# Hybrid block kernel on one core: where g_ffn, the decay weights and two k, q products stand at its start

## The chip, the cores and the metric

The kernel runs on one core of a Trainium2 chip. Its time is in device microseconds (us), the median of several runs. One more execution was taken by the hardware profiler; its time is given beside the median, and all rows below are of that execution. The engines are named TensorE (PE in the rows, PEld for its weight loads), VectorE (DVE), ScalarE (ACT), GpSimd (POOL) and SyncE (SP, which here only issues loads and stores).

## The reference

One layer of a backbone block over 512 latent tokens with a prefix of 256 context tokens, 1024 wide, in float32:

```python
mod_lat = jnp.split(jax.nn.silu(c) @ w_ada[l] + b_ada[l], 6, axis=-1)
mod_ctx = jnp.split(jax.nn.silu(c_ctx)[None, :] @ w_ada[l] + b_ada[l], 6, axis=-1)
pl = project(modulate(rmsnorm(x, g_mix[l]), sh1, sc1), w_in[l], w_dec_up[l], b_dec[l])
pc = project(modulate(rmsnorm(ctx, g_mix[l]), sh1c, sc1c), w_in[l], w_dec_up[l], b_dec[l])
...
zd = jnp.einsum('btdr,drk->dbtk', dd, w_dec_up) + b_dec[:, None, None, :]
log_a = jax.nn.log_sigmoid(zd.astype(jnp.float32)) / DECAY_TAU
...
x = x + gt1[:, None, :] * mix_l
x = x + gt2[:, None, :] * swiglu(modulate(rmsnorm(x, g_ffn[l]), sh2, sc2), w_ffn_in[l], w_ffn_out[l])
return rmsnorm(x, g_final)
```

`project` multiplies the modulated tokens by `w_in`, whose columns are q, k, v, g, the low-rank decay dd (2 x 16 columns), three parts of a short convolution and two branch gates. q, k, v and the decay feed a gated linear attention of 4 heads, scanned in both directions from the context's final states. Its output, gated, and the convolution's are projected, summed and added to x; then comes a SwiGLU sub-layer.

## The kernel before

**Products.** A float32 product is made of three: each operand is split into a rounded high part (`h_...`, a ScalarE copy) and a low part (`l_...`, a VectorE subtraction), and TensorE adds high x high, high x low and low x high (`mm3`). So weights that have landed (`r_...`) pass ScalarE and VectorE before TensorE can take them.

**Order.** From `pinned[0] = True` (L469) up to the end of the attention, the instructions of TensorE, ScalarE and VectorE run in the order of the code; each engine takes its own strictly in turn. Ahead of that line and for the loads, a scheduler sets the order. SP issues the loads. Each has one of eight semaphores in turn, and waits until the earlier load of the same semaphore has landed.

**The start.** Small vectors are loaded as rows of 128 numbers into `vrow` (`small_vectors`, L176): g_mix in rows 0 to 7, g_ffn in 8 to 15, b_ada in 16 to 63, then g_head, b_dec and w_conv up to row 97. A first transpose `vps` (L471) turns rows 0 to 63 into columns of `vec`:

```python
vps = bank("vps")
tr(vps[:, :64], vrow[:64, :P], ident[:64, :64])
dve.tensor_copy(vec[:, :64], vps[:, :64])
normed(0, xts[0])
```

A second one, `vps2` in `head0_gather`, turns the rest. Behind `vps` come the latent tokens: `normed` scales a tile of 128 tokens by its root mean square, `turn` transposes it (`xtp`, TensorE) into `xsT`. Then `ada_rows(0)` multiplies c and c_ctx by the first half of w_ada's shift and scale columns (`ada`, eight tiles `wa` of 512 KB), `mod_cols` turns the row (`adar`) into columns (`adac`, `modT`, `gs`), `warm` does nine products of zeros, and `modulate(f)` makes `h`, tile f of the modulated tokens transposed (eight tiles of 128 channels). `w0_split` splits the weights of head 0 (`r_w`, four sets `wrs` of 256 channels, of which three buffers exist).

**Head 0's gather** (L502) goes through the eight tiles: `gather_v` adds tile k to v and the decay dd of the four latent token tiles, `gather_kq` to k and q. At k = 3 the second half of w_ada (`ada_rows(1)`, 16 loads) comes in, and tiles 4 to 7 are modulated. The context follows in `head0_gather`; there `wdu_split` splits the decay weights `wraw` (w_dec_up, eight loads of 16 rows) into `wdu`.

**Behind it**, `ddt` turns dd into `ddT`, and `decays` multiplies it by `wdu` (the product `z`) and scans the decays. Meanwhile TensorE does `g_tile(0, j)`, in single steps that `fill(n, hd)` puts between the stages. `SPLITS0` names the steps of that fill ahead of which a unit of the next weights is split (`split_unit`; here the two halves of head 1's v weights, `h_v` and `l_v`). The rest (four heads, convolution, projections, SwiGLU) is not touched.

Of the kernel before, what the change touches and what calls it, by code (L numbers as in the profile page):

```python
# [42 lines left out]
R_GM, R_GF, R_BA, R_GH, R_BD, R_WC, R_N = 0, 8, 16, 64, 66, 74, 98  # L43
# [3 lines left out]
def hybrid_block(ctx: ExitStack, tc: tile.TileContext, x, c, ctxt, c_ctx, w_ada, b_ada, g_mix, w_in,  # L47
                 w_dec_up, b_dec, g_head, w_gla_out, w_conv, w_conv_out, w_mix_out, g_ffn,
                 w_ffn_in, w_ffn_out, g_final, out):
    nc = tc.nc  # L50
# [14 lines left out]
    def u2(name, dt=F32, shape=(P, 512)):  # L65
        return up.tile(list(shape), dt, tag="u2", name=name, bufs=NU)
# [17 lines left out]
    def bank(name, shape=(P, 512)):  # L84
        return ps.tile(list(shape), F32, tag="ps", name=name, bufs=3)

    def gbank(name, shape=(P, 512)):
        return ps.tile(list(shape), F32, tag="pg", name=name, bufs=5)
# [17 lines left out]
    def f32(ap):  # L106
        return ap.bitcast(F32)
# [39 lines left out]
    def mm(*a, **k):  # L147
        pe_pin(nc.tensor.matmul(*a, **k))  # L148

    def tr(*a):  # L150
        pe_pin(nc.tensor.transpose(*a))

    def mm3(o, a, b, start, stop):
        mm(o, a[0], b[0], start=start, stop=False)
        mm(o, a[0], b[1], start=False, stop=False)
        mm(o, a[1], b[0], start=False, stop=stop)
# [19 lines left out]
    def small_vectors(vs):  # L176
        for r0, src in vs:
            n = src.shape[1] // P
            for d in range(src.shape[0]):
                nc.sync.dma_start(vrow[r0 + d * n:r0 + (d + 1) * n, :P], src[d:d + 1, :].rearrange("o (r f) -> (o r) f", f=P))  # L180

    small_vectors(((R_GM, g_mix), (R_BA, b_ada)))

    eps = cst.tile([P, 1], F32, name="eps")
    nc.vector.memset(eps, EPS)
# [47 lines left out]
    def token_load(i):  # L233
        if i < NT:
            xt = hp.tile([P, D], F32, tag="xt", name=f"xt{i}", bufs=4)
            nc.sync.dma_start(xt, x[i * P:(i + 1) * P, :])
        else:
            xt = wp.tile([P, D], F32, tag="raw", name=f"xt{i}", bufs=4)
            nc.sync.dma_start(xt, ctxt[(i - NT) * P:(i - NT + 1) * P, :])
        return xt  # L240
# [7 lines left out]
    def turn(i, xt, dst, j):  # L248
        for hh_ in range(2):
            tp = gbank(f"xtp{i}_{hh_}", (P, 4, P))  # L250
            for k in range(4):
                tr(tp[:, k, :], xt[:, (hh_ * 4 + k) * P:(hh_ * 4 + k + 1) * P], ident)
            (act_.copy if hh_ == 0 else dve.tensor_copy)(dst[hh_][:, :, j * P:(j + 1) * P], tp)
# [4 lines left out]
    def ada_load(hf):  # L258

        us = []  # L260
        for k in range(KT):
            src = w_ada[k * P:(k + 1) * P, :2 * D].rearrange("p (s f) -> p s f", s=2)[:, :, hf * 512:(hf + 1) * 512]
            if hf == 1:
                ts = [(uo if s_ else uh)(f"wa{k}{s_}") for s_ in range(2)]
                for s_ in range(2):
                    nc.sync.dma_start(ts[s_], src[:, s_, :])
            else:
                if k % 2 == 0:
                    t = wp.tile([P, 2, 512], F32, tag="raw", name=f"wa0{k}", bufs=4)
                else:  # L270
                    t = hp.tile([P, 2, 512], F32, tag="wa", name=f"wa0{k}", bufs=4)
                nc.sync.dma_start(t, src)
                ts = [t[:, s_, :] for s_ in range(2)]
            us.append(ts)
        return us

    def ada_rows(hf, us):

        rows = gbank(f"ada{hf}")
        for k in range(KT):  # L280
            for s_ in range(2):
                g_ = 64 * (k % 2) + 32 * s_
                mm(rows[g_:g_ + 32, :], cw[:, k, :], us[k][s_], start=k < 2, stop=k >= KT - 2)
        rsb = u2(f"adar{hf}")
        dve.tensor_copy(rsb, rows)
        return rsb
# [5 lines left out]
    def mod_split(src, f, j, hi, lo):  # L292
        g_, sh = gs[:, f, j:j + 1], modT[:, f, 0, j:j + 1]
        act_.activation(hi, src, AF.Identity, scale=g_, bias=sh)
        dve.tensor_scalar(src, src, g_, sh, ALU.mult, ALU.add)
        dve.tensor_sub(lo, src, f32(hi))

    def mod_cols(hf, rsb):
        cp = gbank(f"adac{hf}")
        for i in range(4):  # L300
            mm(cp[:, 4 * i:4 * i + 4], rsb[:, i * P:(i + 1) * P], sel.rearrange("p s c -> p (s c)"), start=True, stop=True)
        fs = slice(4 * hf, 4 * hf + 4)
        ba = vec[:, R_BA:R_BA + 2 * KT].rearrange("p (s f) -> p f s", s=2)
        dve.tensor_tensor(modT[:, fs], cp[:, 0:16].rearrange("p (f s c) -> p f s c", f=4, s=2),
                          ba[:, fs, :].unsqueeze(3).broadcast_to([P, 4, 2, 2]), ALU.add)

        dve.scalar_tensor_tensor(gs[:, fs, :], modT[:, fs, 1, :], 1.0,
                                 vec[:, R_GM + 4 * hf:R_GM + 4 * hf + 4].unsqueeze(2).broadcast_to([P, 4, 2]), ALU.add, ALU.mult)

    def modulate(f):  # L310
        mod_split(xsT[:, f, :], f, 0, *h[f])

    def wdu_load():
        wraw = u2("wraw")
        whi_ = u2("wdhi", F32R)
        for d in range(2):
            for r in range(4):
                nc.sync.dma_start(wraw[d * 64 + r * 16:d * 64 + r * 16 + 16, :], w_dec_up[0, d])
        return wraw, whi_

    def wdu_split(wraw, whi_):
        dve.tensor_copy(whi_, wraw)
        for d in range(2):
            a = d * 64
            dve.tensor_copy(wdu[a:a + 32, :], f32(whi_)[a:a + 32, :])
            dve.tensor_sub(wdu[a + 32:a + 64, :], wraw[a + 32:a + 64, :], f32(whi_)[a + 32:a + 64, :])
# [107 lines left out]
    def w0_load(p_):  # L434

        r = hp.tile([P, 2, NW + 256], F32, tag="wr", name=f"r_w0{p_}", bufs=3)
        for d0, c0, n in ((0, CV, HV), (HV, CD, 32), (NW, CK, P), (NW + P, CQ, P)):
            nc.sync.dma_start(r[:, :, d0:d0 + n], w_in[p_ * 256:(p_ + 1) * 256, c0:c0 + n].rearrange("(a p) b -> p a b", p=P))
        return r

    def w0_at(k, a, e):
        return tuple(w_[:, k % 2, a:e] for w_ in w0[k // 2])

    def gather_v(os, src, k):
        for i, o in enumerate(os):
            mm3(o[:, :NW], tuple(w_[:, i * P:(i + 1) * P] for w_ in src[k]), w0_at(k, 0, NW), k == 0, k == KT - 1)
# [10 lines left out]

    vo = [bank(f"v0_{NC_}")]

    xts = [token_load(i) for i in range(NT)]  # L460
    was = [ada_load(0)]
    wrs = [w0_load(p_) for p_ in range(2)]
    was.append(ada_load(1))
    wrs += [w0_load(p_) for p_ in range(2, 4)]
    small_vectors(((R_GF, g_ffn), (R_GH, g_head), (R_BD, b_dec[0]), (R_WC, w_conv[0])))
    xcs = [token_load(NT + i) for i in range(NC_)]
    wdu_ = wdu_load()
    lat = (xsT[:, :4, :], xsT[:, 4:, :])
    pinned[0] = True  # L469
    vps = bank("vps")  # L470
# [3 lines left out]
    for i in range(NT):  # L474
        if i + 1 < NT:
            normed(i + 1, xts[i + 1])
        turn(i, xts[i], lat, i)
    rsb = ada_rows(0, was[0])
    mod_cols(0, rsb)
    warm(9)  # L480
# [17 lines left out]
    def gather_kq(k):  # L498
        gather(ko, NW, h, k)
        gather(qo, NW + P, h, k)  # L500

    for k in range(KT):  # L502
        if k == 3:
            rsb = ada_rows(1, was[1])
        gather_v(vo, h, k)
        if k == 3:
            mod_cols(1, rsb)
            modulate(4)
            w0_split(2)
            modulate(5)  # L510
            modulate(6)
            w0_split(3)
            modulate(7)
            for i in range(NC_):
                normed(NT + i, xcs[i])
        gather_kq(k)
        if k == 5:
            xcT = [wp.tile([P, 4, TC], F32, tag="raw", name=f"xcT{i}", bufs=4) for i in range(2)]
            for i in range(NC_):
                turn(NT + i, xcs[i], xcT, i)  # L520
            for f in range(KT):
                mod_ctx(f)
# [12 lines left out]
    def head0_gather():  # L535
        for k in range(KT + 2):
            if k < KT:
                gather_v(vc, hc, k)
            if k >= 2:
                gather(kc, NW, hc, k - 2, TC)  # L540
            if k == 5:
                ddt(NC_, NC_ + NT)
                wdu_split(*wdu_)
                vps2 = gbank("vps2")
                tr(vps2[:, :R_N], vrow[:R_N, :P], ident[:R_N, :R_N])
                dve.tensor_copy(vec[:, 64:], vps2[:, 64:R_N])
# [275 lines left out]
    split_unit()  # L822
    head0_ctx()

    SPLITS0 = (3, 7)
    SPLITS = (3, 34, 60, 61)
    SPLITS1 = (25, 34, 60, 61)
    SPLITS3 = (8, 15, 24, 29, 42, 46, 48, 58, 71, 76, 79, 96)
# [2 lines left out]
    def fill(n, hd):  # L831
        nonlocal nwork
        for _ in range(n):
            if nwork in (SPLITS0 if hd < 0 else SPLITS1 if hd == 0 else SPLITS if hd + 1 < H else SPLITS3):
                split_unit()
# [297 lines left out]
    for ch in range(2):  # L1133
# [9 lines left out]
        for t in range(NT):  # L1143
# [8 lines left out]
            else:  # L1152
# [4 lines left out]
                r = rstd_of(ss, 1, D, f"fin{t}")  # L1157
# [32 lines left out]
```

## Time and profile before

| | |
|---|---|
| median of 3 runs (1046.06 to 1047.03) | 1046.06 us |
| the profiled execution's own time | 1044.44 us |
| its span, first to last instruction | 1042.7 us |
| TensorE busy | 985.5 us, 95% of the span |
| VectorE, ScalarE busy | 543.4 us (52%), 382.1 us (37%) |
| GpSimd busy | 2.2 us |
| mean granted TensorE clock | 0.996 |

Busy shares are means over the whole span; a stretch in which an engine stands still is found in the waits and the timeline. In rows, "L102" and "L148" are helpers that record every VectorE and ScalarE operation, or every product, of the pinned part, so the tile's name tells them apart. A row "out<-in" names the tile written and those read. The granted clock is 1.00 at TensorE's higher level (2.4 GHz) and 0.50 at its lower (1.2 GHz).

### The profile page before, as it was taken

What the parts mean: (1) busy time and instruction counts of PE and PEld (TensorE: products, weight loads), DVE (VectorE), ACT (ScalarE), POOL (GpSimd) and SP (SyncE); (2) the same over time, 40 slices, a digit from 0 to 9 for tenths busy, and PEclk for the clock granted to TensorE, in tenths of its full rate; (3) what the DMA queues carried; (4) which work ended last, traced back from release to release, by engine and by line L of the source; (5) the groups of instructions that cost most, each with busy time, mean ns of one, the idle gap of its engine ahead of it and who ended that gap; (6) DMA issues with size and microseconds to landing.
All of it is one profiled execution on the core that took longest, in us unless ns stands there. A gap on an engine that the chain in (4) does not pass through costs nothing.

```text
span 1042.7 us, 12813 instructions
## 1 busy us (share of the span) xinstructions
PE 985.5 (95%) x5204; PEld 823.9 (79%) x5204; DVE 543.4 (52%) x838; ACT 382.1 (37%) x602; POOL 2.2 (0%) x10
## 2 busy tenths in 40 slices
PE   0488999999999999999999999999999999999997
PEld 0267888888788888888888888898888888888886
DVE  1257687677655677778734444743334233332423
ACT  2145656455835422232322232453233232321323
POOL 0000000000000000000000000000000000000000
PEclk9999999999999999999999999999999999999999
DMA  9504111211234667666723222232323323232302
GB/s 322 197 23 112 51 45 58 62 34 49 61 101 132 202 181 223 183 184 200 230 82 105 96 87 99 78 102 83 120 81 101 101 82 118 84 121 81 109 33 81
DMA packets 105536, 117.16 MB, mean 112 GB/s; under 512 B 5395, under 2 KB 89477, under 8 KB 105477
## 3 DMA queue, kind: packets, MB, share of 16 engines
q1 hardware_dynamic: 105476, 116.34, 36.5%
q8 instruction: 41, 0.67, 0.3%
q14 instruction: 19, 0.15, 0.0%
HBM read 114.22 MB, written 2.10 MB: 112 GB/s over the span
## 4 chain that ended last, share of the span: by engine, by line
PE 91%; DMA 3%; ACT 2%; DVE 2%; issue 1%; SPq 0%; ACTq 0%; DVEq 0%
PE f L148 23%; PE fo L148 10%; PE v L148 6%; PE yc L148 4%; PE yg L148 4%; PE gb L148 4%; PE cb L148 4%; PE ch L148 4%; PE cc L148 4%; PE ga L148 4%; PE g L148 4%; PE mx L148 3%; PE kl L148 2%; PE q L148 2%; PE o L148 2%; PE F L148 2%
## 5 line engine op out<-in xcount | busy, mean ns | idle before, releaser
L148 PE MATMUL f<-h,h_fa 128*128 128x512 f32 (+1 forms) x384 | 111.0, 372 | 0.2 <-DVE h L102 0.2
L148 PE MATMUL f<-h,h_fb 128*128 128x512 f32 (+1 forms) x384 | 110.2, 372 | 0.0
L148 PEld LDWEIGHTS f<-h,h_fa 128*128 128x128 f32 x384 | 70.2, 188 | 13.2 <-DVE h L102 0.8
L148 PEld LDWEIGHTS f<-h,h_fb 128*128 128x128 f32 x384 | 70.0, 188 | 12.4
L148 PE MATMUL f<-h,l_fb 128*128 128x512 f32 (+1 forms) x192 | 71.3, 371 | 0.0
L148 PE MATMUL f<-h,l_fa 128*128 128x512 f32 (+1 forms) x192 | 71.3, 371 | 0.0
L102 DVE TENSOR_TENSOR l_fa<-r_fa,h_fa 128x1024 fp32r<-128x1024 f32 x22 | 26.9, 1225 | 74.6 <-ACT h_fa L102 74.6
L102 DVE TENSOR_TENSOR l_fo<-r_fo,h_fo 128x1024 fp32r<-128x1024 f32 x22 | 26.9, 1225 | 68.7 <-ACT h_fo L102 68.7
L148 PE MATMUL fo<-h_fo,ah 128*128 128x512 f32 x154 | 60.5, 393 | 0.0
L148 PE MATMUL fo<-l_fo,ah 128*128 128x512 f32 x154 | 60.5, 393 | 0.0
L148 PE MATMUL fo<-h_fo,al 128*128 128x512 f32 x154 | 60.4, 392 | 0.0
L907 DVE SCALAR_TENSOR_TENSOR acc<-r_wa,c,acc 128x256 f32<-128x256 f32 x112 | 54.1, 483 | 9.9 <-DMA r_wa<-in_w_ada_dram 7.1
L102 ACT CAST h_fo<-r_fo 128x1024 fp32r<-128x1024 f32 x22 | 23.1, 1051 | 71.0 <-PE fo L148 27.4
L148 PEld LDWEIGHTS f<-h,l_fb 128*128 128x128 f32 x192 | 36.2, 188 | 6.3
L148 PEld LDWEIGHTS f<-h,l_fa 128*128 128x128 f32 x192 | 36.1, 188 | 6.3
L148 PE MATMUL g<-h,h_g 128*128 128x512 f32 x128 | 40.9, 401 | 0.0
L148 PE MATMUL gb<-h,h_gb 128*128 128x512 f32 x128 | 40.0, 394 | 0.0
L148 PE MATMUL cb<-h,h_cb 128*128 128x512 f32 x128 | 39.7, 391 | 0.0
L148 PE MATMUL cc<-h,h_cc 128*128 128x512 f32 x128 | 39.6, 390 | 0.0
L148 PE MATMUL ch<-h,h_ch 128*128 128x512 f32 x128 | 39.5, 390 | 0.0
L148 PE MATMUL ga<-h,h_ga 128*128 128x512 f32 x128 | 39.5, 390 | 0.0
L148 PE MATMUL v<-h_v,h 128*128 128x256 f32 x192 | 36.3, 285 | 0.0
(296 smaller groups left out, 2249.2 us busy)
## 6 DMA issues: line engine op xcount, KB each, us to landing
r_wa<-in_w_ada_dram SPq DMA_DIRECT2D x32, 512.0 KB, 4.8
r_fa<-in_w_ffn_in_dram SPq DMA_DIRECT2D x22, 512.0 KB, 3.6
r_fb<-in_w_ffn_in_dram SPq DMA_DIRECT2D x22, 512.0 KB
r_fo<-in_w_ffn_out_dram SPq DMA_DIRECT2D x22, 512.0 KB, 3.6
wa<-in_w_ada_dram SPq DMA_DIRECT2D x8, 512.0 KB, 9.4
wa<-in_w_ada_dram SPq DMA_DIRECT2D x16, 256.0 KB, 4.8
r_g<-in_w_in_dram SPq DMA_DIRECT2D x8, 512.0 KB
r_gb<-in_w_in_dram SPq DMA_DIRECT2D x8, 512.0 KB, 3.8
```

The lines of the kernel that those rows point to most:

```text
L102: return lambda *a, **k: pin(getattr(self.engine, op)(*a, **k))
L148: pe_pin(nc.tensor.matmul(*a, **k))
L907: nc.vector.scalar_tensor_tensor(acc, w_[:, k, :], ck, acc, ALU.mult, ALU.add)
```

## The change

g_ffn is loaded with g_mix and b_ada at the front. The eight loads of w_dec_up are issued by GpSimd instead of SP, called ahead of the tokens' loads, and `wdu_split` stands ahead of the first w_ada product instead of in `head0_gather`. In the gather, k and q of the third tile (k = 2) are done behind v of the fourth. `SPLITS0` moves the two splits by two steps of the fill.

```diff
-    small_vectors(((R_GM, g_mix), (R_BA, b_ada)))
+    small_vectors(((R_GM, g_mix), (R_GF, g_ffn), (R_BA, b_ada)))
...
-                nc.sync.dma_start(wraw[d * 64 + r * 16:d * 64 + r * 16 + 16, :], w_dec_up[0, d])
+                nc.gpsimd.dma_start(wraw[d * 64 + r * 16:d * 64 + r * 16 + 16, :], w_dec_up[0, d])
...
+    wdu_ = wdu_load()
     xts = [token_load(i) for i in range(NT)]
...
-    small_vectors(((R_GF, g_ffn), (R_GH, g_head), (R_BD, b_dec[0]), (R_WC, w_conv[0])))
+    small_vectors(((R_GH, g_head), (R_BD, b_dec[0]), (R_WC, w_conv[0])))
     xcs = [token_load(NT + i) for i in range(NC_)]
-    wdu_ = wdu_load()
...
         turn(i, xts[i], lat, i)
+    wdu_split(*wdu_)
     rsb = ada_rows(0, was[0])
...
         gather_v(vo, h, k)
+        if k == 2:
+            continue
         if k == 3:
             mod_cols(1, rsb)
+            gather_kq(2)
             modulate(4)
...
                 ddt(NC_, NC_ + NT)
-                wdu_split(*wdu_)
...
-    SPLITS0 = (3, 7)
+    SPLITS0 = (5, 9)
```

In SP's queue before, behind the 16 loads of w_ada's second half, stood the third set of head 0's weights, then g_ffn, the other vectors, the decay weights, the context's tokens (`xt`) and the fourth set:

```order
L438 DMA r_w_205<-in_w_in_dram 128x2x256
L438 DMA r_w_205<-in_w_in_dram 128x2x32
L438 DMA r_w_205<-in_w_in_dram 128x2x128 x2
L180 DMA vrow<-in_g_ffn_dram 8x128
L180 DMA vrow<-in_g_head_dram 2x128
L180 DMA vrow<-in_b_dec_dram 4x128 x2
L180 DMA vrow<-in_w_conv_dram 8x128 x3
L318 DMA wraw<-in_w_dec_up_dram 16x512 x8
L239 DMA xt_222<-in_ctx_dram 128x1024
L239 DMA xt_224<-in_ctx_dram 128x1024
L438 DMA r_w_210<-in_w_in_dram 128x2x256
```

Now g_ffn is the fourth load of the program, ahead of b_ada and of the first tokens; the fourth weight set stands right behind the third, and the decay weights are gone from this queue:

```order
L167 DMA c_rows<-in_c_dram 8x128
L168 DMA c_rows<-in_c_ctx_dram 8x128
L180 DMA vrow<-in_g_mix_dram 8x128
L180 DMA vrow<-in_g_ffn_dram 8x128
L180 DMA vrow<-in_b_ada_dram 48x128
L236 DMA xt_150<-in_x_dram 128x1024
```

The front of that queue was the same before but for the g_ffn row. On VectorE, at head 0's decay, the split of the decay weights (`wdhi`, `wdu`) stood ahead of `vec`, g's and head 0's splits, and a v split ahead of the context's ddT:

```order
L102 TENSOR_TENSOR wdu<-wraw,wdhi 32x512
L102 COPY vec<-vps_743 128x34
L102 TENSOR_TENSOR l_g_0_771<-r_g_0_676,h_g_0_770 128x1024
L102 TENSOR_TENSOR l_g_1_778<-r_g_1_678,h_g_1_777 128x1024
L102 TENSOR_TENSOR vl_0_785<-v_0_645,v_0_784 128x256
L102 TENSOR_TENSOR st_136<-v_0_645,ddh_788 128x4x16
L102 TENSOR_TENSOR vl_0_785<-v_1_646,v_0_784 128x256
L102 TENSOR_TENSOR st_136<-v_1_646,ddh_794 128x4x16
L102 TENSOR_TENSOR l_v_0_807<-r_v_0_680,h_v_0_806 128x1024
L102 CAST ddT<-ddt_815 128x256
L102 TENSOR_SCALAR la_820<-z_821,vec 128x256
```

In the changed kernel `vec` follows right behind the latent ddT, and the v split has gone behind the four operations on z (`la`):

```order
L102 CAST ddT<-ddt_737 128x512
L102 COPY vec<-vps_743 128x34
L102 TENSOR_TENSOR l_g_0_771<-r_g_0_681,h_g_0_770 128x1024
L102 TENSOR_TENSOR l_g_1_778<-r_g_1_683,h_g_1_777 128x1024
L102 TENSOR_TENSOR vl_0_785<-v_0_650,v_0_784 128x256
L102 TENSOR_TENSOR st_137<-v_0_650,ddh_788 128x4x16
L102 TENSOR_TENSOR vl_0_785<-v_1_651,v_0_784 128x256
L102 TENSOR_TENSOR st_137<-v_1_651,ddh_794 128x4x16
L102 CAST ddT<-ddt_809 128x256
L102 TENSOR_SCALAR la_814<-z_815,vec 128x256
```

The five operations on the decay weights now stand, on the same engine, between the last copy of the transposed tokens and the copy of the first w_ada row:

```order
L102 COPY xsT<-xtp_1_309 128x4x128
L102 CAST wdhi<-wraw 128x512
L102 CAST wdu<-wdhi 32x512
L102 TENSOR_TENSOR wdu<-wraw,wdhi 32x512
L102 CAST wdu<-wdhi 32x512
L102 TENSOR_TENSOR wdu<-wraw,wdhi 32x512
L102 COPY adar_337<-ada_320 128x512
L102 TENSOR_TENSOR modT<-adac_339,vec 128x16
```

There the copy of the row, and all that follows it, waits behind them for the loads of GpSimd's queue.

## Rows read from the trace of the kernel before

**Rows 1.** The page: busy us (share of the span), instructions.

```profile
PE 985.5 (95%) x5204; PEld 823.9 (79%) x5204; DVE 543.4 (52%) x838; ACT 382.1 (37%) x602; POOL 2.2 (0%) x10
```

**Rows 2.** Waits to 170 us: who, for whom: us, times, longest.

```profile
PE vps L151 <- DMA r_w<-in_w_in_dram: 34.1, 1, 34.1
```

**Rows 3.** Timeline, 0 to 75 us: start, us, instruction [idle before, releaser].

```profile
3.83 0.54 POOL L201 TENSOR_SCALAR_AFFINE_SELECT m<-m 128x128 f32<-128x128 f32 x2
...
7.24 0.29 ACT L102 ACTIVATE rs_x<-ss,eps 128x1 f32<-128x1 f32 x1
...
33.29 0.30 SPq L180 DMA_DIRECT2D vrow<-in_g_ffn_dram  x1
...
37.16 0.34 PE L151 MATMUL vps<-ident,vrow 64*128 64x64 f32 x1 [34.12 <-DMA r_w<-in_w_in_dram]
...
38.67 3.44 PE L151 MATMUL xtp<-ident,xt 128*128 128x128 f32 x16 [1.18 <-DVE xt L102]
...
45.76 3.64 PE L148 MATMUL ada<-wa,cw 128*32 128x512 f32 x32
45.86 0.69 DVE L102 COPY xsT<-xtp 128x512 f32<-128x512 f32 x1 [0.65 <-PE xtp L151]
```

**Rows 4.** Waits of SP's queue up to 130 us.

```profile
SPq L438 <- DMA wa<-in_w_ada_dram: 7.5, 12, 1.0
```

**Rows 5.** Timeline of SP's queue, 20 to 21.5 us.

```profile
20.71 0.37 SPq L438 DMA_DIRECT2D r_w<-in_w_in_dram  x1
```

**Rows 6.** A window: PE, PEld, DVE, ACT, POOL busy, clock, DMA, GB/s.

```profile
10.00:20.00 10.00, 0.00 (x0) 0.00 (x0) 0.00 (x0) 0.00 (x0) 0.00 (x0) 1.00 1.05 388
```

**Rows 7.** The chain that ended last, 40 to 120 us: start, us, what.

```profile
45.83 3.62 PE ada L148 x32
...
55.21 1.72 PE v L148 x11
...
62.89 0.70 PE kl L148 x3
...
69.66 0.80 PE adac L148 x8
...
72.95 1.30 DVE l_w L102
```

**Rows 8.** Timeline, 95 to 107 us: head 0's decay.

```profile
96.02 0.42 DVE L102 CAST wdhi<-wraw 128x512 fp32r<-128x512 f32 x1
...
98.75 0.19 DVE L102 COPY vec<-vps 128x34 f32<-128x34 f32 x1
...
103.52 0.30 PE L151 MATMUL ddt<-ident,st 128*128 128x128 f32 x1 [0.92 <-ACT st L102]
...
104.64 1.23 DVE L102 TENSOR_TENSOR l_v<-r_v,h_v 128x1024 fp32r<-128x1024 f32 x1 [1.27 <-ACT h_v L102]
105.78 0.42 DVE L102 CAST ddT<-ddt 128x256 fp32r<-128x256 f32 x1
...
106.25 0.76 PE L148 MATMUL z<-ddT,wdu 64*128 64x256 f32 x4 [2.43 <-DVE ddT L102]
```

**Rows 9.** Windows ahead of and behind z.

```profile
101.80:106.20 4.40, 0.94 (x4) 0.28 (x2) 2.44 (x5) 2.25 (x7) 0.00 (x0) 1.00 0.82 228
107.00:110.40 3.40, 3.40 (x11) 2.71 (x10) 3.05 (x5) 3.38 (x6) 0.00 (x0) 0.56 0.60 152
```

**Rows 10.** Loads up to 110 us: count, KB each, us to landing.

```profile
wa<-in_w_ada_dram SPq DMA_DIRECT2D x8, 512.0 KB, 9.4
...
wraw<-in_w_dec_up_dram SPq DMA_DIRECT2D x8, 32.0 KB, 1.7
```

**Rows 11.** VectorE's groups to 75 us: count, busy us, mean ns.

```profile
L102 DVE TENSOR_SCALAR xt<-xt,rs_x 128x1024 f32<-128x1024 f32 x4 | 3.0, 753 | 0.1
L102 DVE COPY xsT<-xtp 128x512 f32<-128x512 f32 x4 | 2.8, 688 | 1.9 <-PE xtp L151 1.9
```

## The prediction

> **What bounds the kernel now.** I first read the page's busy times: TensorE works 95% of the span [rows 1], so only a stretch in which it stands still can give back time, and I looked for those. The waits, longest first, have one that stands out: the small transpose `vps` stood 34.1 us [rows 2]. The timeline shows why. TensorE did its first transpose at about 3 us, and `vps` (L471, the first pinned instruction) started at 37.16 [rows 3]; everything pinned on TensorE and VectorE is queued behind it. The waits put this down to `r_w`, the weights of head 0. But `vps` reads only the first 64 rows of `vrow`: g_mix, g_ffn, b_ada. g_mix and b_ada are the third and fourth loads of the program; g_ffn is issued at 33.29 [rows 3], right behind the third `r_w` set in the same queue, whose end releases TensorE at 37.16. A wait for several semaphores is named after the one that changed last, and g_ffn is the only load of that moment that `vps` needs. I take g_ffn to be the late one.
>
> What would be late next? The first w_ada product needs eight tiles of 512 KB. SP keeps eight loads in flight: from the ninth on, each issue waits for the landing of the eighth before it, and L438 waited so for w_ada 12 times [rows 4]. The last piece of the second `r_w` is issued at 20.71 [rows 5], so the eighth w_ada tile had landed at 20.7. The loads stream at 388 GB/s there [rows 6].
>
> The second place is head 0's decay, in the chain of waits [rows 7] and VectorE's timeline [rows 8]: the product `z` starts at 106.25, after TensorE waited 2.43 us for ddT, and before that g had waited for VectorE. VectorE came to it late: from 96.02 to 98.75 it split the decay weights, and at 104.64 it split a value weight ahead of ddT. The windows [rows 9] show what follows: TensorE was busy 0.94 of 4.40 us up to 106.2, and from 107.0 to 110.4 its granted clock was 0.56, mostly the 1.2 GHz level.
>
> **The change, part by part.**
>
> *g_ffn to the front (term A).* The new path to the first product: SP issues one more small load (0.30 [rows 3]) ahead of x and w_ada; the decay weights' eight loads of 32 KB [rows 10] now lie among them, 0.26 MB at 388 GB/s = 0.7 us if all of it is ahead of the eighth tile. So that tile lands at 20.7 + 0.3 + 0.7 = 21.7; the bounds are 21.0 (the bytes fall into gaps) and 21.7, and I take the late one, since the queue is saturated. The transposes don't hold this up: the first ScalarE statistic was ready at 7.24 + 0.29 = 7.5, now 7.85; behind it stand a short reciprocal and the scaling of x, 0.75 [rows 11], so the transposes that started at 38.67 start near 8.8 and, with the same 7.1 us up to the first w_ada product (45.76 [rows 3]), end at 16.0. The product then works off what has landed and finishes an eighth of its 3.62 us [rows 7] behind the last tile: 21.7 + 0.45 = 22.15. Before, it ended at 45.83 + 3.62 = 49.45. A = 27.3 us. The 34.1 us don't come back whole, since 6.8 of them become a wait for w_ada.
>
> From there the path is compute: columns, `modulate`, the split of head 0's weights, and TensorE in full swing at 55.21 [rows 7], now at 27.9. The second half of w_ada was issued ahead of the third `r_w` set, whose end came at 37.16 [rows 3]; it is all there by 38.2, and TensorE wants its last tile near 62.89 - 27.3 + 3.62 = 39.2 [rows 7], the product being as long as the first. Slack of 1 us. The third `r_w`, there by 38.2 too, is wanted only by the split that ends at 74.25 [rows 7], now 45.5. The fourth set now stands ahead of the small vectors in SP's queue and waits for a buffer that is free at 27.9; 0.56 MB at 388 GB/s puts it near 40.
>
> *k, q of the third tile behind the fourth's v (term B).* Before, TensorE did k and q of the third tile (0.70 for k, and q has its shape) and then the second w_ada product; after q of the fourth tile it stood until the split at 74.25 [rows 7]. That chain (w_ada, columns, modulate, split) now begins 1.40 sooner, and the 1.40 of k, q fill its wait (the columns began at 69.66 and took 0.80, k and q behind them 1.40, so the last q ended near 71.9 and about 2.4 us were empty). B = 1.4 us.
>
> *Decay weights split early, the splits at other fills (term C).* VectorE saves 98.75 - 96.02 = 2.73 us ahead of g's and head 0's splits [rows 8]. Behind them the value weight's split with the wait in front of it (1.27 idle from 103.37 on, 1.23 of work) goes behind `z`. ddT of the context then starts when its last transpose is through, 103.52 + 0.30 = 103.8 [rows 8], against 105.78, where `l_v` ends: 1.9 us. C = 2.73 + 1.9 = 4.6 us; both lie on the way to `z`. The moved value splits have until g is through, ten us later.
>
> *The clock behind it (term D).* With C, TensorE stands about 0.7 us there instead of 5, so I expect no fall of the clock: 3.4 us at 0.56 cost 3.4 x 0.44 = 1.5 us. Bounds 0 and 1.5; I take 1.5.
>
> *wraw by GpSimd (cost).* GpSimd's last work ends at 3.83 + 0.54 = 4.4 [rows 3]. The trace has no GpSimd load. Bounds by SP's rows: all eight land 1.7 us after their issue (6.1); one after the other at 1.7 each, 18.0; one after the other at the 9.4 of a w_ada tile, 79.6 [rows 10]. VectorE, now waiting for wraw ahead of the copy of the w_ada row, needs 2.73 for its five operations and is free from about 16.7 (the last copy of x ended at 45.86 + 0.69 [rows 3], 29.85 later than now) to 22.15. So up to a landing at 19.4 it costs nothing; I take at most 18.0, since 32 KB are nearest to their own row. Without that cover it costs 2.7, and more one to one.
>
> Here a rule of the Trainium skill speaks against the change. VectorE works between 5 and 17 us, above all the four scalings and four copies of x, 3.0 + 2.8 us [rows 11]. Its page "SBUF — State Buffer", section "Who interferes with whom", says that GpSimd, which writes the descriptors of its own loads, is blocked out of a shared port while VectorE is in certain fast modes. No run here shows that. The Trainium skill's "DMA: Bandwidth & Descriptors", section "Anatomy of one DMA — SWDGE (gpsimd) path", gives each such load about 2.0 us fixed plus bytes over 436 GB/s; eight in series would by this estimate end at 4.4 + 8 x 2.08 = 21.0, the split at 23.7, which would make the time 1012.9. The row's 1.7 makes it 1011.3.
>
> **Sum.** 27.3 + 1.4 + 4.6 + 1.5 = 34.8 us. The profiled execution took 1044.44 (span 1042.7): 1009.6. The median of the runs shown is 1.62 above it: 1046.06 - 34.8 = **1011.3 us**. Behind head 0 the engines' order is the same as before, and TensorE has the 95% of [rows 1] there too, so I let the rest move as a block. Own range 1008.5 to 1013: half a us for A's bounds, half of D and what runs differ (1046.06 to 1047.03).
>
> **Rivals.**
> 1. *The clock falls at the start* (0.13). From 17.8 to 22.2 TensorE gets 0.45 us of w_ada work per tile, every 1.35 us: a third busy. The 0.94 of 4.40 ahead of the slow stretch [rows 9] speaks for it, the nine warm-up products just before the first real one against it. Price: the last w_ada step, the columns and one stretch like the 1.5 us of D, 1.5 to 3 us: 1013 to 1014.3.
> 2. *GpSimd's loads are late* (0.10). If they go one after the other and also lose the 5.8 us of VectorE [rows 11], wraw is there at 23.8, the split ends at 26.5 and the w_ada row is 4.4 late: 1015.7. For it: a load engine never used here, beside a saturated queue; against: 15 us to do it in. This is also what the rule of the Trainium skill's page "SBUF — State Buffer" would do.
> 3. *`vps` waited for something else* (0.03), as the name in [rows 2] says: then A is gone and B + C + D remain, less 1.0 for the added loads: 1039.6. Against it: `vps` does not read `r_w`.
> 4. *Slower* (0.03): wraw served behind each w_ada tile, 9.4 us apiece, lands at 79.6 and its split ends at 82.3, against 49.45 before: 32.9 later, less B + C + D = 7.5, so 1071. It decides from a landing at 54.3, 6.2 us a load.
>
> The forecast has 0.70; 0.01 is left for no change. 1008 to 1018 takes in the forecast and rivals 1 and 2. Within 0.2% counts as the same, about what a measurement can tell here; by these cases faster has 0.96, same 0.01, slower 0.03.
>
> **What would show it.** `vps` at about 4 us; the first w_ada product from 16, ending near 22, waiting for w_ada; wraw landed before 19; TensorE dense from about 28; the second w_ada product at 35.5 with no long wait for a load; `z` near 106.25 - 27.3 - 1.4 - 4.6 = 72.9, with the clock at 1.00 behind it. The forecast is wrong if the copy of the w_ada row waits for VectorE's split, if the clock is 0.5 around 28, or if a wait for `r_w` or w_ada stands behind 36.

## The result and the profile after

The changed kernel takes 1012.05 us (median of 4 runs, 1011.44 to 1013.26) against 1046.24 (1046.06 to 1047.03): a ratio of 0.9673, 95% interval 0.9656 to 0.9690. Forecast were 1011.3, with a range of 1008 to 1018. The profiled execution took 1012.35 us (span 1010.6), where the sum gave 1009.6. TensorE is busy 98% of the span, in the page's line of busy us:

```profile
PE 986.5 (98%) x5204; PEld 823.4 (81%) x5204; DVE 543.3 (54%) x838; ACT 382.1 (38%) x602; POOL 6.4 (1%) x18
```

The timeline of the kernel after (start in us, duration, instruction, idle time before it and its releaser) answers to [rows 3, 7, 8]:

```profile
4.00 0.34 PE L151 MATMUL vps<-ident,vrow 64*128 64x64 f32 x1 [0.92 <-DMA vrow<-in_b_ada_dram]
...
4.32 4.33 POOL L318 DMA_DIRECT2D wraw<-in_w_dec_up_dram  x8
...
17.04 0.69 DVE L102 COPY xsT<-xtp 128x512 f32<-128x512 f32 x1 [0.65 <-PE xtp L151]
17.65 0.42 DVE L102 CAST wdhi<-wraw 128x512 fp32r<-128x512 f32 x1
...
23.85 1.05 PE L148 MATMUL ada<-wa,cw 128*32 128x512 f32 x4 [0.31 <-DMA wa<-in_w_ada_dram]
24.95 0.69 DVE L102 COPY adar<-ada 128x512 f32<-128x512 f32 x1 [4.61 <-PE ada L148]
...
30.70 0.40 PE L148 MATMUL v<-l_w,h 128*128 128x288 f32 x1 [1.12 <-DVE l_w L102]
...
42.07 0.69 DVE L102 COPY adar<-ada 128x512 f32<-128x512 f32 x1 [6.66 <-PE ada L148]
...
47.00 1.28 DVE L102 TENSOR_TENSOR l_w<-r_w,h_w 128x1088 fp32r<-128x1088 f32 x1
48.34 0.40 PE L148 MATMUL v<-l_w,h 128*128 128x288 f32 x1 [0.84 <-DVE l_w L102]
...
75.69 0.62 PE L148 MATMUL z<-ddT,wdu 64*128 64x256 f32 x4 [0.52 <-DVE ddT L102]
```

Four points lay the gain out, each against its time before. TensorE is dense (from its first product with `l_w` on, it has work without long waits) from 30.70 (55.21 in [rows 7]): 24.5 us earlier. The split that the third set of weights waits for ends at 47.00 + 1.28 = 48.28 (74.25): 26.0 earlier, so 1.5 more. `z` starts at 75.69 (106.25): 30.6 earlier, 4.6 more. The span is 32.1 shorter: 1.5 more, behind `z`, where the clock no longer falls:

```profile
75.40:83.00 7.60, 7.31 (x34) 5.92 (x35) 4.44 (x8) 6.84 (x10) 0.00 (x0) 1.00 0.34 82
```

(A window: busy us of PE, PEld, DVE, ACT, POOL, then granted clock, DMA share, GB/s; [rows 9] has 0.56 there.) So B, C and D came out as forecast, and A, 27.3 in the forecast, is 2.8 short. The loads show where; these rows answer to [rows 10]:

```profile
wa<-in_w_ada_dram SPq DMA_DIRECT2D x8, 512.0 KB, 12.1
...
wraw<-in_w_dec_up_dram POOLq DMA_DIRECT2D x8, 32.0 KB, 6.2
```

A w_ada tile takes 12.1 us to land, where it took 9.4. The first product begins its last tile at 23.85, where the sum had that tile landed at 21.7, and ends at 24.9, not at 22.15: the tile is 2.15 us late, and its four products take 1.05 where the sum had 0.45.

### The profile page after: what moved, and what is told of

Same layout as the page of the kernel before. It is cut to its first block, busy times and chain, and to the rows that moved or that the text cites. A ratio compares the mean times of both kernels' runs of the same rounds, so it can differ in the third digit from the quotient of the medians.

```text
span 1010.6 us, 12827 instructions
## 1 busy us (share of the span) xinstructions
PE 986.5 (98%) x5204; PEld 823.4 (81%) x5204; DVE 543.3 (54%) x838; ACT 382.1 (38%) x602; POOL 6.4 (1%) x18
## 4 chain that ended last, share of the span: by engine, by line
PE 93%; DMA 2%; ACT 2%; DVE 2%; issue 0%; SPq 0%; ACTq 0%; DVEq 0%
PE f L148 24%; PE fo L148 11%; PE v L148 6%; PE yc L148 4%; PE yg L148 4%; PE gb L148 4%; PE cb L148 4%; PE g L148 4%; PE ch L148 4%; PE cc L148 4%; PE ga L148 4%; PE mx L148 3%; PE kl L148 2%; PE q L148 2%; PE o L148 2%; PE F L148 2%
## 5 line engine op out<-in xcount | busy, mean ns | idle before, releaser
L102 DVE TENSOR_TENSOR l_fa<-r_fa,h_fa 128x1024 fp32r<-128x1024 f32 x22 | 26.9, 1225 | 74.6 <-ACT h_fa L102 74.6
L1125 DVE TENSOR_TENSOR sil<-sil,f 128x512 f32<-128x512 f32 x22 | 15.1, 687 | 39.5 <-PE f L148 39.5
## 6 DMA issues: line engine op xcount, KB each, us to landing
wa<-in_w_ada_dram SPq DMA_DIRECT2D x8, 512.0 KB, 12.1
```

The source lines that it names most:

```text
L102: return lambda *a, **k: pin(getattr(self.engine, op)(*a, **k))
L1125: nc.vector.tensor_mul(sil, sil, obs[2 + j])
```

## The experiments

Of the twelve runs, the first eight ask where the 2.8 us went, the last four what each part is worth. The kernels:

- *g_ffn alone*: the kernel before with `(R_GF, g_ffn)` in the front list.
- *late by SyncE*, *ahead of the second half*, *two loads there*: the changed kernel with the lines below (the places of `wdu_load` and the number of loads differ; the comments are not in the code).
- *among w_ada*: the changed kernel with one 32 KB load by SyncE behind each of the eight first w_ada tiles, and the split at k = 3 as below.
- *two GpSimd loads*, *sixteen GpSimd loads*, *by ScalarE*: the same place as in the changed kernel, by the second set of lines (one for each; in *two loads there* the line is SyncE's).

```
-    wdu_ = wdu_load()                       # ahead of x
...
-                nc.gpsimd.dma_start(wraw[d * 64 + r * 16:d * 64 + r * 16 + 16, :], w_dec_up[0, d])
+                nc.sync.dma_start(wraw[d * 64 + r * 16:d * 64 + r * 16 + 16, :], w_dec_up[0, d])
...
     was = [ada_load(0)]
     wrs = [w0_load(p_) for p_ in range(2)]
+    wdu_ = wdu_load()                       # "ahead of the second half"
     was.append(ada_load(1))
+    wdu_ = wdu_load()                       # or here: "late by SyncE"
...
-    wdu_split(*wdu_)
     rsb = ada_rows(0, was[0])
...
         if k == 3:
+            wdu_split(*wdu_)
             rsb = ada_rows(1, was[1])
```

```
+            nc.gpsimd.dma_start(wraw[d * 64:d * 64 + 64, :], w_dec_up[0, d].unsqueeze(0).broadcast_to([4, 16, 512]))
...
+                nc.gpsimd.dma_start(f32(whi_)[d * 64 + r * 16:d * 64 + r * 16 + 16, :], w_dec_up[0, d])
                 nc.gpsimd.dma_start(wraw[d * 64 + r * 16:d * 64 + r * 16 + 16, :], w_dec_up[0, d])
...
+                nc.scalar.dma_start(wraw[d * 64 + r * 16:d * 64 + r * 16 + 16, :], w_dec_up[0, d])
```

What they gave (us; "dense" is the start of the first product with `l_w`, "second row" the start of VectorE's copy of the second w_ada row, `z` its start; these three are from the one profiled execution, the times are medians of 4 or 5 runs). In *g_ffn alone* 1.40 us of k and q still stand ahead of the second row. The kernel before, run beside each group, had medians of 1046.14 to 1047.05, so times that differ by less than about 1 us don't tell two kernels apart. Behind each time below stands its ratio to that kernel, with its 95% interval.

| loads of the decay weights | dense | second row | z | time |
|---|---|---|---|---|
| changed kernel: 8, GpSimd, front | 30.70 | 42.07 | 75.69 | 1012.05 |
| g_ffn alone: 8, SyncE, last | 27.97 | 40.77 | 79.57 | 1018.61 |
| late by SyncE: 8 | 27.94 | 41.54 | 74.89 | 1012.03 |
| ahead of the second half: 8 | 28.02 | 41.63 | 75.25 | 1012.15 |
| two loads there | 28.90 | 41.51 | 75.05 | 1011.94 |
| among w_ada: 8, SyncE | 30.37 | 41.73 | 75.25 | 1011.90 |
| 2, GpSimd, front | 31.09 | 42.49 | 76.02 | 1013.67 |
| 16, GpSimd, front | 32.51 | 43.91 | 77.42 | 1014.75 |
| 8, ScalarE, front | 35.18 | 46.55 | 80.06 | 1017.07 |

**g_ffn alone.**

> The kernel before with g_ffn alone moved to the front; the decay weights stay SyncE's last loads, the order of k, q and the splits stay as before. In the changed kernel TensorE was dense from 30.7 us, 24.5 earlier than before, where 27.3 were forecast; the eighth w_ada tile was some 2.5 us late. T1: GpSimd's queue costs the stream of loads more than its 0.26 MB. T2: these small loads cost it, by whichever queue. T3: the stream is slowed by TensorE, ScalarE and VectorE working on x beside it, whatever GpSimd does. By T1 and T2 the stream stays at about 388 GB/s from 10 to 14 us (it was 298 and 329 in the changed kernel), TensorE is dense from 27.2 to 27.9 and the time is 1046.2 less 27.3 to 28.0, 1018.2 to 1018.9. By T3 it is dense from about 30 (less the 0.7 of the bytes) and the time is 1021.0. In any case the wait for ddT and the fall of the clock to 0.56 behind z are still there.

1018.61 (ratio 0.9732, 0.9716 to 0.9748), dense from 27.97: T1 and T2 hold, T3 falls. Here are four windows of this kernel, then the same of the changed kernel, columns as above:

```profile
8.00:10.00 2.00, 1.13 (x6) 1.14 (x7) 1.52 (x4) 1.16 (x3) 0.00 (x0) 1.00 1.01 401
10.00:12.00 2.00, 2.00 (x11) 2.00 (x11) 0.87 (x2) 1.95 (x5) 0.00 (x0) 1.00 1.05 401
12.00:14.00 2.00, 1.52 (x8) 1.12 (x7) 1.66 (x4) 1.80 (x4) 0.00 (x0) 1.00 1.05 395
14.00:16.00 2.00, 1.86 (x17) 1.48 (x18) 1.47 (x3) 0.96 (x2) 0.00 (x0) 1.00 1.05 385
```

```profile
8.00:10.00 2.00, 0.15 (x1) 0.16 (x2) 0.92 (x2) 1.94 (x6) 0.65 (x2) 1.00 1.02 384
10.00:12.00 2.00, 2.00 (x10) 2.00 (x11) 1.07 (x3) 1.18 (x3) 0.00 (x0) 1.00 1.07 298
12.00:14.00 2.00, 1.52 (x9) 1.12 (x7) 1.52 (x4) 1.97 (x5) 0.00 (x0) 1.00 1.06 329
14.00:16.00 2.00, 1.32 (x9) 1.12 (x10) 1.67 (x4) 1.35 (x4) 0.00 (x0) 1.00 1.05 374
```

From 10 to 14 us TensorE, VectorE and ScalarE work on x in both, and without GpSimd's loads the stream keeps 395 to 401 GB/s. With them it falls to 298, though the DMA engines' share stays at 1.07: they are as busy and move less. The last tile of the first product, in *g_ffn alone*:

```profile
21.12 1.05 PE L148 MATMUL ada<-wa,cw 128*32 128x512 f32 x4 [0.30 <-DMA wa<-in_w_ada_dram]
```

Without these loads term A's sum has that tile at 21.0 and TensorE dense at 27.2. The tile came at 21.1 and dense at 27.97: what the sum lacks here is in the tile's four products, which took 1.05 us and not 0.45.

**Late by SyncE.**

> The changed kernel, but the decay weights are loaded by SyncE behind the second half of w_ada, and split while the second w_ada product runs. T1 and T2: the 2.8 us that the first product lost come back, dense from 27.9, time 1012.05 - 2.8 = 1009.3. T3: only the 0.7 us of the bytes come back, 1011.3. If the split (2.7 us on VectorE) comes too late for the copy of the second w_ada row, up to 2.7 us are lost again: 1012.

1012.03 (0.967, 0.9655 to 0.9685): the start gave the 2.8 us back, dense from 27.94, and the next stage took them. VectorE, of this kernel:

```profile
38.80 0.43 DVE L102 CAST wdhi<-wraw 128x512 fp32r<-128x512 f32 x1 [6.16 <-DMA wraw<-in_w_dec_up_dram]
...
41.54 0.69 DVE L102 COPY adar<-ada 128x512 f32<-128x512 f32 x1
```

The decay weights landed at 38.8, so the copy of the second row, whose product ended at 39.2, stood behind their split until 41.54. TensorE waited 1.29 us, and from 43 to 47 us its clock was 0.57, mostly the 1.2 GHz level:

```profile
43.00:47.00 4.00, 4.00 (x14) 3.18 (x14) 2.67 (x5) 3.21 (x4) 0.00 (x0) 0.57 0.98 325
```

**By ScalarE.**

> The changed kernel with the eight loads of the decay weights issued by ScalarE in place of GpSimd, at the same time (about 3 to 7.3 us), the same bytes in the same pieces. T1 (GpSimd's queue is what costs): 2.1 of the 2.8 us come back, the 0.7 of the bytes stay: 1010.0, dense from 28.6. T2 (the small loads cost, whichever queue) and T3 (the engines' work): no change, 1012, dense from 30.7. If ScalarE's first statistic comes later by the issues, that is no cost, since the transposes have some 1 us to wait for loads.

1017.07 (0.9721, 0.9705 to 0.9737), a miss that tells T1 from T2 by nothing, since another wait took over. Timeline of this kernel, ScalarE and its queue:

```profile
8.05 8.02 ACTq L318 DMA_DIRECT2D wraw<-in_w_dec_up_dram  x6
16.12 1.06 ACT L102 ACTIVATE junk<-xt 128x1024 bf16<-128x1024 f32 x1 [10.95 <-DMA wa<-in_w_ada_dram]
```

The last six issues took until 16.07, and the wait ended with the landing of a w_ada tile; so ScalarE's loads seem to share the eight semaphores of SyncE's. The first statistic of x, next on ScalarE, came at 16.12 instead of 7.33. "No cost" in the expectation was wrong by 8.8 us on ScalarE, 4.5 on the path.

**Sixteen GpSimd loads.**

> The changed kernel with GpSimd loading the decay weights twice (first into the tile that their rounded copy later takes): sixteen loads of 32 KB, 0.52 MB. T1 and T2: the cost beyond the bytes doubles as well, the first product ends 2.8 us later again, 1014.9, dense from 33.5. T3: only the bytes count, 0.7 us: 1012.7. If the loads come one after the other at 1.7 us and more, the split is late and the row's copy waits for it: 1016 and more.

1014.75 (0.9696, 0.968 to 0.9713), 2.70 more than the changed kernel, the number of T1 and T2; but dense came at 32.51, 1.8 later and not 2.8, and the profiled execution took 1014.05, 1.70 more than that of the changed kernel. The other 1.0 of the median lies in executions that have no profile. The split began at 21.87 and its five operations ended near 24.6; the copy of the first w_ada row waited for the product, not for it. The stream ran at 297 GB/s until 22 us (g_ffn alone: 388 from 16 to 20), in a window of this kernel:

```profile
16.00:22.00 6.00, 3.31 (x19) 0.61 (x20) 0.82 (x2) 0.23 (x1) 0.00 (x0) 0.96 1.06 297
```

**Among w_ada.**

> The changed kernel with the decay weights loaded by SyncE, one 32 KB load behind each of the eight w_ada tiles, the same bytes in the same pieces as GpSimd's, and their split in VectorE's wait for the second w_ada product. T1 (it is GpSimd's own queue beside SyncE's that slows the stream): only the 0.7 us of the bytes stay, dense from 28.6, 1010.0. T2 (the small loads by whichever queue): dense from about 30.7 and 1012.0.

1011.90 (0.9667, 0.9651 to 0.9683), dense from 30.37: T2, and T1 falls. First this kernel, then the one with late loads, the same twelve us:

```profile
10.00:22.00 12.00, 9.85 (x55) 5.74 (x56) 4.91 (x9) 4.92 (x10) 0.00 (x0) 1.00 1.05 345
```

```profile
10.00:22.00 12.00, 10.06 (x61) 4.97 (x59) 4.62 (x9) 4.80 (x10) 0.00 (x0) 1.00 1.06 378
```

At the same share SyncE's own small loads take the stream from 378 to 345 GB/s, 0.4 MB less in 12 us with their 0.26 MB counted as moved.

**Ahead of the second half.**

> The changed kernel with the decay weights loaded by SyncE ahead of the second half of w_ada (in the run before this they were behind it, landed at 38.8 and their split held up the second w_ada row by 2.3 us), and split by VectorE ahead of the second row, in its wait from 32.6 to 39. T2 and T1 (these loads, beside the first w_ada tiles, cost the 2.8 us): dense from 27.9, second product at 35.6, its row copied at 39.2 without a wait for the split, z at 72.9, time 1012.05 - 2.8 = 1009.3. T4 (the 2.8 us can't come back since the next stretch then waits for the later loads, second half of w_ada or third set of head 0's weights): up to 1012.

(The run that this text compares with is *late by SyncE*.) 1012.15 (0.9672, 0.9655 to 0.9689): dense from 28.02, and again nothing left of it. The split ran from 32.64 to 35.3 without a wait; what was late is the second half of w_ada. Two windows of this kernel, then the product in its timeline:

```profile
24.00:27.00 3.00, 2.42 (x11) 0.96 (x11) 1.81 (x5) 2.36 (x3) 0.00 (x0) 1.00 0.43 97
27.00:32.00 5.00, 3.98 (x25) 3.71 (x26) 4.90 (x8) 2.57 (x4) 0.00 (x0) 1.00 0.90 282
```

```profile
35.63 5.96 PE L148 MATMUL ada<-wa,cw 128*32 128x512 f32 x32
```

Here the share falls with the rate, 0.43 and 97 GB/s: too little was asked for. SyncE issued the eight 32 KB loads from 22.01 to 25.59, one every 0.45 us, which is 73 GB/s, and the stream ran at 68 and 78 GB/s from 25 to 27; only 0.6 of these 3.58 us were waits for an earlier load. The product, 3.64 us long in the changed kernel, waited for tiles for the difference: T4.

**Two loads there.**

> As the run with the decay weights ahead of the second half of w_ada, by SyncE, but in two loads of 128 KB in place of eight of 32 KB. There eight small loads were all that was in flight, the stream fell to 68 to 145 GB/s from 24 to 27 us and the second w_ada product took 5.96 us in place of 3.64. T7 (eight loads are in flight at most, so small ones starve the stream): with two the stream stays above 250 GB/s from 24 to 28, the product ends at 39.3, z at 72.9, time 1012.05 - 2.8 = 1009.3. T8 (the bytes ahead of the second half delay it, whatever their number): the product still ends past 41, 1012.

1011.94 (0.9671, 0.9653 to 0.9689). The number that T8 gave. T7 is half right: the stream fell less (176 GB/s from 24 to 27) but under the 250 that T7 forecast, and the product waited 1.35 us for tiles in place of 2.3, of which 0.26 MB at 378 GB/s would be 0.7. The rest of its late end is a start 0.9 later: dense at 28.90, though its first stage has the same loads as the three kernels that were dense at 27.9 to 28.0. Windows and product of this kernel:

```profile
24.00:27.00 3.00, 2.98 (x17) 1.66 (x17) 0.93 (x4) 1.48 (x2) 0.00 (x0) 1.00 0.64 176
27.00:32.00 5.00, 3.50 (x20) 3.03 (x21) 4.90 (x8) 3.45 (x5) 0.00 (x0) 1.00 0.99 313
```

```profile
36.48 4.99 PE L148 MATMUL ada<-wa,cw 128*32 128x512 f32 x32
```

**Two GpSimd loads.**

> The changed kernel with the decay weights loaded by GpSimd in two loads of 128 KB (each reading one direction's 32 KB four times over) in place of eight of 32 KB: the same place, queue, bytes and rows. What is known by now: eight loads cost the start 2.76 us by GpSimd, 2.4 by SyncE among the w_ada tiles, sixteen 4.6, so about 0.3 us a load, of which 0.08 are bytes. T5 (the number of loads counts): six fewer give back 6 x 0.22 to 0.26 = 1.3 to 1.6 us, dense from 29.1 to 29.4, 1010.5 to 1010.8. T6 (the bytes, or their 2 KB pieces beside SyncE's, count): dense from 30.7, 1012.0.

1013.67 (0.969, 0.9671 to 0.9708), dense from 31.09: T5 falls, two loads cost as much as eight or more. T6's 1012.0 isn't met either. The number was not varied by itself, though: by the trace's packet records GpSimd's two loads went out as 64 packets of 4 KB and 224 of 4 or 8 bytes, its eight as 128 of 2 KB and 128 of 4 bytes. Windows of this kernel:

```profile
10.00:12.00 2.00, 2.00 (x11) 2.00 (x10) 0.96 (x2) 1.85 (x5) 0.00 (x0) 1.00 1.07 223
12.00:14.00 2.00, 1.44 (x11) 1.10 (x10) 1.56 (x4) 1.97 (x6) 0.00 (x0) 1.00 1.06 213
```

**g_ffn put back.** The changed kernel with `(R_GF, g_ffn)` moved from the front list to the head of the late one.

> The changed kernel with g_ffn alone put back to its old place behind the third set of head 0's weights. If g_ffn is what the small transpose waited for: it starts at about 38 to 40 (37.16 before, later by the 0.7 to 2.8 us of GpSimd's loads), and what is left are the 7.6 us of k and q, of the decay split and of the clock: 1046.2 - 7.6 + 0.7 to 2.8 = 1039.3 to 1041.4. If it waited for something else the start stays as in the changed kernel: 1012. If the other parts only count because the start is early: 1046 and more.

1038.93 (0.9927, 0.9913 to 0.9940), a little under the expected range, which went by the median of the kernel before. From profile to profile the sum holds: 1044.44 - 7.5 + 2.35 (dense at 57.56 for 55.21) = 1039.3, and the profiled execution took 1039.26. g_ffn is what `vps` waits for, in this kernel's timeline:

```profile
39.49 0.34 PE L151 MATMUL vps<-ident,vrow 64*128 64x64 f32 x1 [36.40 <-DMA vrow<-in_w_conv_dram]
```

The name in this row is once more not the cause: `vps` reads neither `r_w`, named in [rows 2], nor w_conv; both are just the load that changed last. From dense (57.56) to `z` (102.58) it is 45.02 us, in the changed kernel 44.99: the other parts don't depend on the start.

**k and q put back.**

```
-        if k == 2:
-            continue
         if k == 3:
             mod_cols(1, rsb)
-            gather_kq(2)
```

> The changed kernel with k and q of the third tile back ahead of the second w_ada product. If their 1.40 us fill TensorE's wait for the third set's split there: 1012.05 + 1.4 = 1013.5. If the wait would have been as short without them, or is given back later: 1012.

1013.30 (0.9684, 0.9666 to 0.9701), 1.25 more. In its profiled execution (1014.30) the second row came 42.49 - 29.72 = 12.77 us behind dense, in the changed kernel 42.07 - 30.70 = 11.37: 1.40, the moved work. That execution lost 1.5 more to the clock behind the wait that k and q fill in the changed kernel; three of its five runs are at 1013.1 to 1013.3. The window behind the wait:

```profile
48.00:52.00 4.00, 3.24 (x13) 3.12 (x14) 3.93 (x6) 3.97 (x7) 0.00 (x0) 0.65 0.01 4
```

**The splits at 3 and 7.** `SPLITS0 = (3, 7)` in place of `(5, 9)`.

> The changed kernel with the two splits of head 0's fills back at 3 and 7 in place of 5 and 9. If the value split ahead of ddT kept z waiting, as in the kernel before: z 1.9 us later, 1014.0, and up to 1.5 more if TensorE's clock falls behind that wait, 1015.5. If the decay split's 2.73 us alone made z early and ddT waits for its transposes anyway: 1012.

1014.91 (0.9701, 0.968 to 0.9721), 2.9 more. In its profiled execution (1013.23) `z` came 76.54 - 29.75 = 46.79 us behind dense, 1.80 later than with the change, after a wait of 2.32 us, and the clock held at 1.00 behind it:

```profile
76.54 0.62 PE L148 MATMUL z<-ddT,wdu 64*128 64x256 f32 x4 [2.32 <-DVE ddT L102]
```

So 1.8 us are the wait; that the rest, seen in the median, is a clock that falls in some executions is argued, not shown.

**The decay split put back.** `wdu_split(*wdu_)` again behind `ddt` in `head0_gather`.

> The changed kernel with the split of the decay weights back where it was in head 0's gather, loads as in the changed kernel. If VectorE's chain is the path there: z 2.7 us later, 1014.8, and 1.5 more if the clock falls behind the wait, 1016.3. If it is covered by TensorE's work: 1012. The start must not change (the split waited for nothing there): dense from 30.7, give or take 1.

1015.75 (0.9706, 0.9687 to 0.9725), 3.7 more. `z` came 78.11 - 30.41 = 47.70 us behind dense, 2.71 later, and the clock fell behind it, in a window of this kernel:

```profile
78.00:82.00 4.00, 3.89 (x12) 2.88 (x13) 2.59 (x6) 3.25 (x6) 0.00 (x0) 0.57 0.27 74
```

The clock cost 4 x 0.43 = 1.7 us at most; its profiled execution took 1016.31, which is 1012.35 + 2.71 - 0.29 (dense earlier) + 1.54.

## Why the prediction was right, and where it was off

**The late load.** Right. `vps` starts at 4.00, and with g_ffn put back 26.9 us of the gain are lost again (1038.93 - 1012.05); g_ffn alone is worth 27.6 (1046.24 - 1018.61). Rival 3 is out.

**Term A, mis-sized: 24.5 for 27.3.** Two of its steps failed. The first is "0.26 MB at 388 GB/s = 0.7 us": the decay weights' loads cost the stream nearly three times that. Without those loads dense came at 27.94, 27.97, 28.02 and 28.90 in four kernels. With them it came at 30.70, and in the three kernels with the same start (k and q, the splits, the decay split put back) at 29.72, 29.75 and 30.41. The means are 28.2 and 30.1, a cost of 1.9 us, 1.2 more than the sum had. The second is "an eighth of its 3.62 us": the last tile's products took 1.05 us in each of these kernels, 0.6 more than the 0.45 of the sum, which took a product that runs through for one that waits for its tile. The remaining 1.0 of the 2.8 is what starts differ by from one execution to the next: the changed kernel's profile lies 0.6 behind the mean of its group, and without the loads the last tile came at 21.1 in three kernels, where the sum has 21.0, but at 22.05 in the fourth. The way from the end of that product to dense took 5.8 us, as before. The product itself began at 16.93, where the sum had 16.0; that cost nothing, since it waited for tiles.

The packet records of the traces show where the 1.9 us go. For x and the first eight w_ada tiles, the packets took 16.7 to 17.1 us of each of the 16 DMA engines (a mean) in the four kernels without these loads; with GpSimd's eight, its packets counted, they took 18.7 to 19.0 in the four others. Of the 2.0 us between the means 0.95 are GpSimd's own packets. The rest is that SyncE's packets take longer beside them: from 10 to 12 us a w_ada packet of 2 KB took a median of 109 to 118 ns in these four, 84 in those without, and 162 beside GpSimd's two loads; from 14 to 20, when GpSimd's packets were through, it took 88 again.

What it is not: GpSimd's queue (SyncE's own loads among w_ada: dense at 30.37), or the engines' work on x (395 to 401 GB/s beside it). Fewer loads don't help by themselves (two of 128 KB: 31.09). In all of these the DMA share is full and the rate low. Why loads into 16 or 64 rows that read the same 32 KB four times slow the packets beside them stays open; neither the rows nor the repeated source was varied.

**Why moving them gained nothing.** The second w_ada row needs its tiles and, in these kernels, VectorE free of the decay split. Loaded ahead of the second half the weights make a hole in the stream, loaded behind it they are late for VectorE, and loaded among the first tiles they are as dear as GpSimd's. In each case the second row is copied at 41.5 to 41.7 and the time is 1012; that these different waits end so close together is chance. *g_ffn alone*, which has the loads last, copies that row at 40.77 with 1.40 us of k and q ahead of it, so at 39.4 without them. A version with the weights behind the second half and their split past head 0's weights might keep 2 to 3 us; it wasn't tried.

**Terms B, C, D.** Measured 1.5, 4.6 and 1.5 in the profiled execution, as forecast; B and C put back by themselves show their sizes (1.40 for k and q, 2.71 for the decay split, 1.80 for the value split). D shows in the spans behind `z`: from its start to the end it is 936.3 to 936.5 us in the three kernels whose clock fell right behind it (the kernel before, g_ffn alone, the decay split put back), 934.9 to 935.6 in the eleven where it held. In the 7.5 us ahead of `z` TensorE stood 4.5 us before and 0.6 in the changed kernel, near the 5 and 0.7 of the sum.

**Rivals 1, 2 and 4.** The clock was 1.00 from 16 to 25 us in the changed kernel. With k and q put back, which leaves the code up to there as it is, the profiled execution had 0.63 from 14 to 18 and was dense at 29.72 all the same. With sixteen loads it had 0.50 from 22 to 24, and the last tile's products began only at 25.66, with the clock at 1.00 again. The product waits for loads there, so rival 1's fall happened in two of these profiles and cost nothing that shows.

GpSimd's loads landed in time, so rivals 2 and 4 are out: the split follows the last copy of x at 17.65 with no wait. The eight were issued in 4.33 us and took 6.2 each (a median), overlapping. The estimate in series from the Trainium skill's "DMA: Bandwidth & Descriptors", section "Anatomy of one DMA — SWDGE (gpsimd) path", 21.0, isn't met.

In the changed kernel VectorE's work on x could not hold GpSimd up: the last issue ended at 8.65 and the first scaling of x began at 9.04. With sixteen loads GpSimd issued from 4.33 to 15.88, partly beside VectorE's work on x. Of its fourteen issues from 5.82 on, eleven took 0.48 or 0.49 us; three took 0.74, 0.62 and 0.96 and ended 0.10 us behind a scaling. GpSimd and VectorE, of this kernel:

```profile
8.08 0.75 DVE L102 TENSOR_SCALAR xt<-xt,rs_x 128x1024 f32<-128x1024 f32 x1
8.19 0.74 POOL L319 DMA_DIRECT2D wraw<-in_w_dec_up_dram  x1
...
13.97 0.96 POOL L319 DMA_DIRECT2D wraw<-in_w_dec_up_dram  x1
14.08 0.75 DVE L102 TENSOR_SCALAR xt<-xt,rs_x 128x1024 f32<-128x1024 f32 x1
```

So the block of the Trainium skill's "SBUF — State Buffer", section "Who interferes with whom", shows in these three issues, and cost them 0.9 us together. Three other issues that lie in part beside a scaling took 0.48 or 0.49. GpSimd's three gaps there (1.19, 0.96, 0.36) end with its own earlier loads.

**The median.** 0.75 off, where the sum is 2.8 off: the profiled execution of before lay 1.6 below the median that the offset was taken from, that of after 0.3 above its own. The two misses partly cancel: that the median came within 1 us of the forecast is luck.

## What to carry to other kernels

When one transpose or product waits for a set of small loads, ask which of them is issued last, not which name the wait carries: here one load of 4 KB behind a queue of weights cost 27 us. Bytes added to a saturated load stream are not priced by its rate alone; compare the DMA share with the GB/s (full share and low rate: the loads themselves are slow; both low: too little was asked for), and look whether the next stage hangs on the same stream before moving them. A last step that waits for its load is priced as it runs alone, not as its share of a run without waits. A wait that is taken away ahead of dense products can be worth its length and half as much again, where the clock then holds (2.71 and 1.54 us for the decay split here).

## What the runs showed of the hardware

- 0.26 MB of loads into 16 or 64 rows each, beside 512 KB tiles: from 10 to 14 us the stream fell from 395 to 401 GB/s to 213 to 329 at a DMA share of 1.06 to 1.07, by GpSimd's queue; a 2 KB packet of the tiles took 109 to 162 ns in place of 84 (10 to 12 us). By SyncE's queue the stream fell from 378 to 345 (10 to 22 us).
- Six loads that ScalarE issued beside SyncE's took 8.02 us to issue, up to the landing of a w_ada tile, and all of ScalarE's work stood behind them. GpSimd's eight waited for none of SyncE's.
- Eight loads of 32 KB issued by SyncE one every 0.45 us made a stream of 68 to 78 GB/s.
- The same start ran at a clock of 1.00 from 14 to 18 us in the changed kernel's profile and at 0.63 in that with k and q put back. Behind waits of 2.4 us ahead of `z` the clock fell in two profiles (0.56 in the kernel before, 0.65 in g_ffn alone from 80 to 84 us), behind one of 2.3 us (splits at 3 and 7) it stayed at 1.00.
